# The gate stage dealt out anew and the last stage run tile by tile in a Griffin, sparse-attention and PEER layer

## The chip, the cores and the metric

The kernel runs on one core of a Trainium2 chip. The metric is the time of one execution in device microseconds (us), as the median of several runs. The engines have queues of their own, served in order: TensorE (PE: matrix products into PSUM; PEld is its weight load), VectorE (DVE), ScalarE (ACT: activation functions, copies), GpSimd (POOL) and SyncE (SP, which here only issues transfers). One engine waits for another only through semaphores.

## The reference

One decoder layer over 512 tokens of width 1024, in float32, cut here to the parts around the change:

```
xa  = causal_dwconv(z_rx) + b                      # 4 taps
r   = sigmoid(xa @ w_r + b_r);  ig = sigmoid(xa @ w_i + b_i)     # 8 diagonal blocks of 128
a   = exp(-8 r softplus(-lam))
u   = sqrt(1 - a^2) * (ig * xa)                    # "gate product": ig * xa
h_t = a_t h_(t-1) + u_t                            # scan over the tokens
y_a = (h * gelu(z_rg)) @ w_a
kc, vc = two-layer MLP over blocks of 32 tokens, hidden width 256    # compressed keys, values
...                                                # attention, merge, PEER expert FFN
gate = sigmoid(rmsnorm(h) @ ple_wg)
h    = h + gate * (p @ ple_wp)
out  = rmsnorm(h) * g_final
```

## The kernel before

Every matrix product is made of three (`mm3`): both operands are split into a high part (a copy, rounded) and a low part (the value less its high part), and high x high, high x low and low x high are summed in PSUM. So each weight tile costs a copy and a subtraction before TensorE may use it (`split`, lines 124 to 129: the high part on ScalarE unless an engine is given, the low part on VectorE or GpSimd).

The order of the work is written by hand: the program emits instructions in the order of the Python code, and each engine runs its own in that order. Four stages matter here.

1. **Gate stage, rx chunks (line 398).** Eight chunks of 128 columns of `z_rx`, 24 products each, and then two of `z_kc`. `ev_rx` evacuates a chunk: the convolution on ScalarE (`xa`, line 380) and three VectorE steps (line 382), the splits of the gate weights (`lwhl`) and of `xa` (`xhl`). It hands back `gates`, which `gemm` calls behind the products of the next chunk and ahead of that chunk's evacuation: six products, two sigmoids, and the gate product `gx * xa` (line 395).
2. **Gate stage, rg and vc chunks (lines 547 to 564).** Ten chunks, 24 products each. Between them stand the 32 steps of the compression MLP, 16 for keys and 16 for values (`compress`, lines 480 to 508, products `hid`), at the places that the table `CSTEP` gives: by chunk, the numbers k after which a step comes. Their weights come 256 KB at a time through four buffers (`w1_load`, issued by GpSimd), are cast on ScalarE (`w1_split`, line 455) and get their low half on VectorE (`w1_lo`, line 464), which in turn lets the load four steps on start. `SIDE` gives the places of the work that TensorE does not wait for at once: `lru_b` (tanh and two exponentials), `lru_sqrt`, `lru_c` (product and scan) and the sine and cosine for the rotary embedding.
3. **vs and vw (lines 578 to 605).** The value projections; the last seven steps of the MLP stand in the first of them. `lru_d` follows in the side list.
4. **Last stage (lines 1501 to 1525).** After the expert sums (`va`, in PSUM) the four tiles of 128 tokens are added to the residual (`fin_a`), normalised (`fin_n`), transposed (`fin_t`), multiplied with `ple_wg` in two halves of 512 columns (`fin_mm`, weights `wg0`, `wg1`), gated (`fin_post`), and normalised again for the output (`fin_c`, and by hand for tile 2, which is last). Tile 3 (`GT`) comes first; its part of the FFN was computed by gathers.

Of the kernel before, what the change touches and what calls it, by code (L numbers as in the profile page):

```python
# [94 lines left out]
def tile_hybrid(ctx, tc, a, out, dbg=None):  # L95
# [480 lines left out]
    for br, n in enumerate(("vs", "vw")):  # L576
        hl = hls[br]
        os = [bank("v") for _ in range(NT)]
        for i in range(NT):
            ts = slice(i * 128, (i + 1) * 128)  # L580
            for k in range(KD):
                T.matmul(os[i][:, :256], nhi[:, k, ts], hl[0][:, k], start=k == 0, stop=False)
                T.matmul(os[i][:, :256], nlo[:, k, ts], hl[0][:, k], start=False, stop=False)
# [15 lines left out]
        for i in range(NT):  # L599
# [818 lines left out]
    def fin_post(i, hf, o):
        c = slice(hf * 512, (hf + 1) * 512)
        sgm = wp2.tile([128, 512], F32, name="sgm", tag="sgm", bufs=2)  # L1420
        A.activation(sgm, o, AF.Sigmoid)
# [184 lines left out]
```

## Time and profile before

| | us |
|---|---|
| three runs | 1884.24, 1883.34, 1878.03 |
| their median | 1883.34 |
| the profiled execution | 1883.07 |
| its span, first to last instruction | 1881.3 |
| TensorE busy in the span | 1811.3 (96%) |
| VectorE, ScalarE, GpSimd busy | 1405.0, 840.0, 643.6 |

The span is cut below into stretches by what TensorE does: the rx and kc chunks (24.94 to 90.88 us from its start), rg chunks 0 to 5 with the key MLP (to 137.61), the vc chunks and rg 6 and 7 (to 173.08), vs and vw (to 202.44), everything up to the last expert product (to 1820.69), and the last stage. In rows with brackets the bracket is the idle time of that engine just before the instruction, and what ended it. "x4" is a run of four instructions, and its time is that of all four.

### The profile page before, as it was taken

The page shows a single profiled execution, that of the slowest core. Times are in us where ns is not written, and L with a number is a line of the kernel's source. Part 1 is how long each engine was busy: PE and PEld are TensorE (multiplying, and loading weights), DVE is VectorE, ACT ScalarE, POOL GpSimd, SP SyncE. Part 2 cuts the span into 40 slices and gives each one's busy share as a digit, 9 for nine tenths or more (in the row PEclk, how much of TensorE's full clock was granted, in tenths as well). Part 3 has the DMA queues.
Part 4 walks back from the last instruction along what each step waited for, and adds up shares of the span by engine and source line. Part 5 has one row for each costly group of instructions (what it writes and reads, how often), then busy time and mean ns, then how long its engine had stood idle before and what let it go on. Part 6 is the DMA issues. An engine that isn't in the chain of part 4 may idle for free.

```text
span 1881.3 us, 26477 instructions
## 1 busy us (share of the span) xinstructions
PE 1811.3 (96%) x9817; PEld 1586.6 (84%) x9817; DVE 1405.0 (75%) x2628; ACT 840.0 (45%) x1274; POOL 643.6 (34%) x417
## 2 busy tenths in 40 slices
PE   7998999999999989899999999999999999999997
PEld 6777888778789889899999888888888899999986
DVE  6867616766634388999999957888787788888864
ACT  4464323445522344674765753333333333333443
POOL 3311444322135315435335312222222355555400
PEclk9999999999999999999999999999999999999999
DMA  4353232211015436796897989999999899999941
GB/s 172 102 178 108 79 112 68 68 57 46 23 67 191 181 117 215 260 353 240 293 343 249 355 322 316 356 352 357 344 358 347 306 337 324 354 337 346 358 179 45
DMA packets 179810, 433.29 MB, mean 230 GB/s; under 512 B 14560, under 2 KB 88032, under 8 KB 179680
## 3 DMA queue, kind: packets, MB, share of 16 engines
q1 hardware_dynamic: 119664, 241.96, 37.4%
q0 software_dynamic: 40288, 145.77, 21.8%
q10 hardware_dynamic: 19728, 43.86, 6.1%
q8 instruction: 77, 1.26, 0.3%
q14 instruction: 53, 0.43, 0.1%
HBM read 382.25 MB, written 49.28 MB: 229 GB/s over the span
## 4 chain that ended last, share of the span: by engine, by line
PE 70%; DVE 16%; ACT 4%; issue 4%; DMA 4%; POOL 0%; SPq 0%; DVEq 0%; ACTq 0%; POOLq 0%
PE va L134 9%; PE va L133 9%; PE va L132 9%; PE xu L134 7%; PE xu L132 7%; PE xu L133 7%; DVE ul L1101 2%; DVE oh L1273 2%; DVE gr L1302 2%; PE G L1250 1%; DVE P L769 1%; DMA w1buf<-in_cmp_w 1%; DVE acc L1308 1%; PE z_w_a L134 1%; PE z_w_b L133 1%
## 5 line engine op out<-in xcount | busy, mean ns | idle before, releaser
L132 PE MATMUL xu<-x2hi,uh 128*128 128x384 f32 x1008 | 344.3, 342 | 4.5 <-ACT ac L1111 4.5
L134 PE MATMUL xu<-x2hi,ul 128*128 128x384 f32 x1008 | 339.9, 337 | 6.5 <-DVE ul L1101 6.5
L133 PE MATMUL xu<-x2lo,uh 128*128 128x384 f32 x1008 | 339.2, 337 | 0.0
L132 PE MATMUL va<-v,A 128*128 128x512 f32 x768 | 299.0, 389 | 1.5 <-ACT A L126 1.5
L134 PE MATMUL va<-v,A 128*128 128x512 f32 x768 | 298.9, 389 | 0.0
L133 PE MATMUL va<-v,A 128*128 128x512 f32 x768 | 298.9, 389 | 0.0
L1287 POOL DMA_INDIRECT gr<-in_peer_u,eidx x128 | 170.2, 1329 | 329.5 <-DVE gr L1302 251.7
L1287 POOL DMA_INDIRECT gr<-in_peer_v,eidx x128 | 187.1, 1461 | 268.1 <-DVE acc L1308 210.4
L126 ACT CAST v<-vring 128x1024 fp32r<-128x1024 f32 x128 | 134.7, 1052 | 263.3 <-issue 157.2
L129 DVE TENSOR_TENSOR v<-vring,v 128x1024 fp32r<-128x1024 f32 x128 | 156.4, 1222 | 68.6 <-ACT v L126 68.2
L134 PEld LDWEIGHTS xu<-x2hi,ul 128*128 128x128 f32 x1008 | 190.6, 189 | 7.8 <-DVE ul L1101 7.8
L132 PEld LDWEIGHTS xu<-x2hi,uh 128*128 128x128 f32 x1008 | 190.7, 189 | 6.7 <-ACT ac L1111 5.1
L133 PEld LDWEIGHTS xu<-x2lo,uh 128*128 128x128 f32 x1008 | 190.8, 189 | 1.6
L134 PEld LDWEIGHTS va<-v,A 128*128 128x128 f32 x768 | 144.1, 188 | 30.3 <-DVE A L129 0.6
L132 PEld LDWEIGHTS va<-v,A 128*128 128x128 f32 x768 | 144.1, 188 | 30.2 <-ACT A L126 1.8
L133 PEld LDWEIGHTS va<-v,A 128*128 128x128 f32 x768 | 144.2, 188 | 28.5 <-DVE v L129 0.3
L1308 DVE SCALAR_TENSOR_TENSOR acc<-gr,dots,acc 128x1024 f32<-128x1024 f32 x128 | 163.8, 1280 | 1.6
L1302 DVE SCALAR_TENSOR_TENSOR gr<-gr,x2g 128x1024 f32<-128x1024 f32 x128 | 158.0, 1254 | 8.2 <-DMA gr<-in_peer_u,eidx 8.2
L1096 ACT CAST uh<-ur 128x1024 fp32r<-128x1024 f32 x126 | 132.6, 1053 | 57.3 <-ACT ac L1111 29.7
L1111 ACT ACTIVATE ac<-xu 128x384 f32<-128x384 f32 x128 | 63.7, 498 | 191.7 <-PE xu L134 181.8
L1101 DVE TENSOR_TENSOR ul<-ur,uh 128x1024 fp32r<-128x1024 f32 x100 | 121.4, 1220 | 17.6 <-PE xu L134 8.3
L1253 ACT ACTIVATE gst<-G 128x512 f32<-128x512 f32 x96 | 100.3, 1158 | 13.5 <-PE G L1250 13.2
(449 smaller groups left out, 3599.5 us busy)
## 6 DMA issues: line engine op xcount, KB each, us to landing
vring<-in_peer_v SPq DMA_DIRECT2D x128, 512.0 KB
ur<-in_peer_uT SPq DMA_DIRECT2D x126, 512.0 KB
gdram<-gst ACTq DMA_DIRECT2D x12, 2048.0 KB
gt<-gdram SPq DMA_DIRECT2D x32, 768.0 KB
xdram<-ac ACTq DMA_DIRECT2D x88, 192.0 KB
vring<-xdram SPq DMA_DIRECT2D x88, 192.0 KB
raw_m<-in_w_in SPq DMA_DIRECT2D x16, 512.0 KB
raw_rx<-in_w_in SPq DMA_DIRECT2D x8, 512.0 KB
```

The costliest lines, as they stand in the source:

```text
L126: A.copy(hi, src)
L129: (eng or V).tensor_tensor(lo, src, f(hi), op=OP.subtract)
L132: T.matmul(o, sh, mh, start=start, stop=False)
L133: T.matmul(o, sh, ml, start=False, stop=False)
L134: T.matmul(o, sl, mh, start=False, stop=stop)
L1096: A.copy(us[e][0], urs[e])
L1101: (G if search[0] else V).tensor_tensor(us[e][1], urs.pop(e), f(us[e][0]), op=OP.subtract)
L1111: A.activation(ac, o[:, :ND], AF.Gelu_apprx_tanh)
L1253: A.activation(gst[:, :, c:c + 4].rearrange("p a t -> p t a"), o.rearrange("p (t a) -> p t a", t=4), AF.Copy, scale=1.0 / GSC)
L1287: G.indirect_dma_start(out=r, out_offset=None, in_=tab, in_offset=bass.IndirectOffsetOnAxis(ap=eidx[:, j:j + 1], axis=0))
L1302: V.scalar_tensor_tensor(r, r, 1.0, x2g, op0=OP.mult, op1=OP.mult, accum_out=dots[:, j:j + 1])
L1308: V.scalar_tensor_tensor(acc, r, dots[:, j:j + 1], acc, op0=OP.mult, op1=OP.add)
```

## The change

The gate product is no longer part of `gates`: it is put in a list `late`, which the next chunk's `ev_rx` empties behind its own convolution and splits (the last one goes into the side list). `CSTEP` and `SIDE` are new tables. At the end of a chunk that is followed by one with MLP steps, the low halves of all weights cast so far are made. In the last stage the four steps add, statistic, normalise and transpose go tile by tile, with the last quarter of `wg1`'s second half split between the tiles; the square root's table is loaded ahead; tile 0 is transposed after the fourth of eight steps of the product before it and not after the seventh; and tile 2's last product is made in two of 256 columns, with the multiplication by `g_final` ahead of the last statistic.

```diff
+    late = []
...
-        split(wh[:, 0], wh[:, 1], w, G, V)
-        split(xh[:, 0], xh[:, 1], xa)
+        A.copy(xh[:, 0], xa)
+        V.tensor_copy(wh[:, 0], w)
+        V.tensor_tensor(xh[:, 1], xa, f(xh[:, 0]), op=OP.subtract)
+        G.tensor_tensor(wh[:, 1], w, f(wh[:, 0]), op=OP.subtract)
+        while late:
+            late.pop(0)()
 
         def gates():
...
-            V.tensor_tensor(gx[:, c], gx[:, c], xa, op=OP.mult)
+            late.append(lambda: V.tensor_tensor(gx[:, c], gx[:, c], xa, op=OP.mult))
         return gates
...
+    side.insert(0, lambda: late.pop(0)())
...
-    gemm([("kc", i, nhi, nlo, ev_kv(0)) for i in range(2)], nside=(2, 1), nxt=[("rg", 0), ("rg", 1)])
+    gemm([("kc", i, nhi, nlo, ev_kv(0)) for i in range(2)], nside=(3, 1), nxt=[("rg", 0), ("rg", 1)])
...
-    CSTEP = [(), (), (1, 3, 5, 7), (1, 3, 5, 7), (1, 3, 5, 7), (0, 2, 3, 5, 7), (), (), (4, 5, 6, 7), (0, 1, 3, 4, 6, 7)]
-    SIDE = [(5,), (), (), (0, 0), (0, 0), (1,), (0, 0, 4), (0, 3, 6), (1, 2, 5), (1, 4, 6)]
+    CSTEP = [(), (), (1, 3, 5, 7), (1, 3, 5, 7), (1, 3, 5, 7), (0, 2, 3, 5, 7), (), (), (1, 6, 7), (0, 1, 2, 4, 5, 6, 7)]
+    SIDE = [(5,), (), (), (2, 4), (2, 4), (2,), (0, 0, 3, 6), (3, 6), (7, 7), (5,)]
...
             run_side(SIDE[n].count(k))
+            if k == 7 and CSTEP[n + 1:n + 2] != [()]:
+                w1_lo(w1n[1])
...
                 if br == 0 and k % 4 == 3:
                     next(comp, None)
+                if br == 0 and i < 3 and k == 5:
+                    run_side(1)
...
-            run_side(1)
+            run_side(1 + br)
...
-            if mid is not None and k == 6:
+            if mid is not None and k == midk:
                 mid()
...
-            w_half(wg1, 1, raw_p7)
+            for k in range(0, KD - 2, 2):
+                w_part(wg1, 1, k, raw_p7)()
+            wcut = w_part(wg1, 1, KD - 2, raw_p7)
+            A.activation(rms[:, 3, 1:2], rms[:, 2, 1:2], AF.Sqrt)
...
-    for i in range(GT):
-        fin_a(i)
-    fin_n(range(GT))
-    og = [fin_mm(GT, 0, "o"), fin_mm(GT, 1, "f", lambda: fin_t(0, ("ax", "ax")))]
+    fin_a(0)
+    fin_a(1)
+    rms_fin(0, 1)
+    fin_a(2)
+    apply3(0)
+    rms_fin(1, 2)
+    wcut()
+    apply3(1)
+    rms_fin(2, 3)
+    apply3(2)
+    og = [fin_mm(GT, 0, "o"), fin_mm(GT, 1, "f", lambda: fin_t(0, ("ax", "ax")), 3)]
...
+    ends = [(0, 512), (512, 768), (768, 1024)]
+    for n, (c0, c1) in enumerate(ends):
+        fin_post(2, c0 // 512, fin_mm(2, c0 // 512, cols=(c0 % 512, (c1 - 1) % 512 + 1)), (c0, c1))
+        if n == 2:
+            A.activation(rms[:, 3, 1:2], rms[:, 2, 1:2], AF.Sqrt)
+        A.activation(last[:, c0:c1], h2[:, c0:c1], AF.Square, accum_out=sq[:, n:n + 1])
+        if n == 1:
+            V.tensor_tensor(sq[:, 0:1], sq[:, 0:1], sq[:, 1:2], op=OP.add)
+        V.tensor_tensor(h2[:, c0:c1], h2[:, c0:c1], gF[:, c0:c1], op=OP.mult)
+    V.tensor_tensor(sq[:, 2:3], sq[:, 2:3], sq[:, 0:1], op=OP.add)
     rms_fin(2, 3)
+    A.activation(last[:, :512], h2[:, :512], AF.Copy, scale=rms[:, 3, 2:3])
+    V.tensor_scalar(last[:, 512:], h2[:, 512:], rms[:, 3, 2:3], None, op0=OP.mult)
```

First place: VectorE in the rx chunks, from one weight cast (`w`, for a chunk two ahead) to the split of `xa`. Before:

```order
L128 CAST w_555<-raw_kc 128x1024
L395 TENSOR_TENSOR gx<-gx,xa 128x512
L382 SCALAR_TENSOR_TENSOR xa<-z_rx,par,xa 128x511
L382 SCALAR_TENSOR_TENSOR xa<-z_rx,par,xa 128x510
L382 SCALAR_TENSOR_TENSOR xa<-z_rx,par,xa 128x509
L128 CAST lwhl<-lruw 128x256
L129 TENSOR_TENSOR xhl<-xa,xhl 128x512
```

Now:

```order
L128 CAST w_555<-raw_kc 128x1024
L384 SCALAR_TENSOR_TENSOR xa<-z_rx,par,xa 128x511
L384 SCALAR_TENSOR_TENSOR xa<-z_rx,par,xa 128x510
L384 SCALAR_TENSOR_TENSOR xa<-z_rx,par,xa 128x509
L390 CAST lwhl<-lruw 128x256
L391 TENSOR_TENSOR xhl<-xa,xhl 128x512
L401 TENSOR_TENSOR gx<-gx,xa 128x512
```

The gate product of the chunk before has moved from ahead of the convolution to behind the split.

Second place: VectorE where the MLP steps begin (rg chunk 2) and go on (chunk 3); `w` are the weights of a chunk two ahead, `w1hl` the MLP's low halves, `tt` the vector part of `lru_b`. Before:

```order
L129 TENSOR_TENSOR w_819<-raw_rg,w_819 128x1024
L128 CAST w_850<-raw_rg 128x1024
L129 TENSOR_TENSOR w_850<-raw_rg,w_850 128x1024
L464 TENSOR_TENSOR w1hl<-w1buf,w1hl 128x512 x2
L464 TENSOR_TENSOR w1hl<-w1half,w1hl 128x512 x2
L464 TENSOR_TENSOR w1hl<-w1buf,w1hl 128x512
L128 CAST w_915<-raw_rg 128x1024
L129 TENSOR_TENSOR w_915<-raw_rg,w_915 128x1024
L410 SCALAR_TENSOR_TENSOR tt<-a_805,tt 128x512
L410 SCALAR_TENSOR_TENSOR tt<-a_922,tt 128x512
L464 TENSOR_TENSOR w1hl<-w1buf,w1hl 128x512
```

Now:

```order
L129 TENSOR_TENSOR w_819<-raw_rg,w_819 128x1024
L471 TENSOR_TENSOR w1hl<-w1buf,w1hl 128x512
L128 CAST w_852<-raw_rg 128x1024
L129 TENSOR_TENSOR w_852<-raw_rg,w_852 128x1024
L471 TENSOR_TENSOR w1hl<-w1buf,w1hl 128x512
L471 TENSOR_TENSOR w1hl<-w1half,w1hl 128x512 x2
L471 TENSOR_TENSOR w1hl<-w1buf,w1hl 128x512 x2
L128 CAST w_917<-raw_rg 128x1024
L129 TENSOR_TENSOR w_917<-raw_rg,w_917 128x1024
L417 SCALAR_TENSOR_TENSOR tt<-a_805,tt 128x512
L471 TENSOR_TENSOR w1hl<-w1half,w1hl 128x512
L417 SCALAR_TENSOR_TENSOR tt<-a_935,tt 128x512
```

One low half now stands ahead of each chunk's weight cast and subtraction, and the `tt` steps stand between low halves and not ahead of them.

Third place: VectorE at the program's end, tile 2's last 512 columns and the output. Before:

```order
L1422 TENSOR_TENSOR sgm<-sgm,ppb 128x512
L1423 TENSOR_TENSOR h<-h,sgm 128x512
L1520 TENSOR_TENSOR rms<-rms 128x1
L286 TENSOR_SCALAR rms<-rms 128x1
L287 RECIPROCAL rms<-rms 128x1
L1524 SCALAR_TENSOR_TENSOR x3s<-h,rms,gfinB 128x512 x2
```

Now (from the product with `g_final` of the first 512 columns on):

```order
L1549 TENSOR_TENSOR h<-h,gfinB 128x512
L1434 TENSOR_TENSOR sgm<-sgm,ppb 128x256
L1435 TENSOR_TENSOR h<-h,sgm 128x256
L1548 TENSOR_TENSOR rms<-rms 128x1
L1549 TENSOR_TENSOR h<-h,gfinB 128x256
L1434 TENSOR_TENSOR sgm<-sgm,ppb 128x256
L1435 TENSOR_TENSOR h<-h,sgm 128x256
L1549 TENSOR_TENSOR h<-h,gfinB 128x256
L1550 TENSOR_TENSOR rms<-rms 128x1
L286 TENSOR_SCALAR rms<-rms 128x1
L287 RECIPROCAL rms<-rms 128x1
L1553 TENSOR_SCALAR x3s<-h,rms 128x512
```

Six instructions have become twelve; the two fused output steps have become products ahead of the statistic and one scaling behind it, with the other half of the scaling on ScalarE.

## Rows read from the trace of the kernel before

**Rows 1.** The busy time by stretch: bounds in us, length, busy time of PE, PEld, DVE, ACT and POOL (instructions), granted TensorE clock, share of the DMA engines, GB/s.

```profile
24.94:90.88 65.94, 62.48 (x265) 49.08 (x264) 54.28 (x104) 28.62 (x41) 27.38 (x20) 1.00 0.35 111
90.88:137.61 46.73, 42.27 (x210) 34.44 (x209) 31.65 (x45) 31.95 (x49) 9.12 (x17) 1.00 0.57 177
137.61:173.08 35.47, 30.02 (x137) 24.23 (x136) 31.37 (x42) 19.07 (x26) 3.97 (x8) 0.90 0.35 109
...
202.44:1820.69 1618.25, 1586.40 (x8704) 1400.89 (x8702) 1228.81 (x2342) 712.96 (x1074) 585.05 (x359) 1.00 0.70 248
1820.69:1836.66 15.97, 12.68 (x59) 9.96 (x58) 10.71 (x16) 8.27 (x12) 0.00 (x0) 1.00 0.37 145
1871.06:1881.30 10.24, 0.16 (x1) 0.00 (x0) 4.66 (x9) 3.62 (x9) 0.00 (x0) 0.64 0.26 102
```

**Rows 2.** The timeline of TensorE in the rx and kc chunks: start, duration, engine, line, operation, shapes, count.

```profile
24.94 0.39 PE L132 MATMUL z_rx<-nhi,w 128*128 128x512 f32 x1
...
30.38 0.39 PE L132 MATMUL lru<-xhl,lwhl 128*128 128x512 f32 x1
...
60.77 0.49 PE L132 MATMUL lru<-xhl,lwhl 128*128 128x512 f32 x1 [1.21 <-ACT xhl L126]
61.62 0.50 PE L133 MATMUL lru<-xhl,lwhl 128*128 128x512 f32 x1 [0.36 <-DVE xhl L129]
```

**Rows 3.** The timeline of GpSimd (one row, a low half of `w`) and VectorE in the same chunks.

```profile
54.84 2.40 POOL L129 TENSOR_TENSOR w<-raw_rx,w 128x1024 fp32r<-128x1024 f32 x1 [2.76 <-DVE w L128]
...
54.88 2.91 DVE L395 TENSOR_TENSOR gx<-gx,xa 128x512 f32<-128x512 f32 x1
57.71 2.30 DVE L382 SCALAR_TENSOR_TENSOR xa<-z_rx,par,xa 128x511 f32<-128x511 f32 x3
...
76.52 2.13 DVE L270 SCALAR_TENSOR_TENSOR ang<-kt,ang 128x512 f32<-128x512 f32 x3
...
79.63 0.68 DVE L395 TENSOR_TENSOR gx<-gx,xa 128x512 f32<-128x512 f32 x1
```

**Rows 4.** The timeline of TensorE and VectorE in rg chunk 2.

```profile
104.57 0.62 PE L491 MATMUL hid<-w1hl,blk 128*124 128x256 f32 x3 [1.16 <-DVE w1hl L464]
108.26 0.64 PE L491 MATMUL hid<-w1hl,blk 128*124 128x256 f32 x4
110.11 0.64 PE L491 MATMUL hid<-w1hl,blk 128*124 128x256 f32 x4
...
103.83 1.28 DVE L464 TENSOR_TENSOR w1hl<-w1buf,w1hl 128x512 fp32r<-128x512 f32 x2
```

**Rows 5.** The busy time of rg chunks 3 and 4, from one gelu on ScalarE to the next (columns as in Rows 1; ScalarE's is the fourth busy time).

```profile
110.50:121.10 10.60, 9.28 (x48) 7.31 (x47) 7.04 (x11) 9.83 (x16) 2.68 (x5) 1.00 0.51 149
121.10:131.66 10.56, 8.59 (x46) 6.80 (x45) 6.17 (x9) 9.33 (x15) 2.15 (x4) 1.00 0.53 161
```

**Rows 6.** The timeline around the MLP's weight loads: the issue on GpSimd, the casts and the gelu on ScalarE.

```profile
104.81 1.14 POOL L449 DMA_DIRECT2D w1buf<-in_cmp_w  x2 [18.79 <-DVE w1hl L464]
...
109.31 1.29 ACT L455 CAST w1hl<-w1buf 128x512 fp32r<-128x512 f32 x2 [5.21 <-DMA w1buf<-in_cmp_w]
...
120.60 0.60 ACT L527 ACTIVATE gr<-z_rg 128x512 f32<-128x512 f32 x1
```

**Rows 7.** The timeline of TensorE and VectorE around rg chunk 6, where the MLP for the values begins.

```profile
154.47 0.74 PE L491 MATMUL hid<-w1hl,blk 128*124 128x256 f32 x4 [1.27 <-DVE blk L129]
...
159.06 1.00 PE L491 MATMUL hid<-w1hl,blk 128*124 128x256 f32 x3 [3.04 <-DVE w1hl L464]
...
141.71 0.69 DVE L420 TENSOR_TENSOR gx<-gx,tt 128x512 f32<-128x512 f32 x1 [1.94 <-ACT tt L415]
142.43 1.23 DVE L421 TENSOR_TENSOR_SCAN rr<-rr,gx 128x512 f32<-128x512 f32 x1
...
158.34 0.67 DVE L464 TENSOR_TENSOR w1hl<-w1buf,w1hl 128x512 fp32r<-128x512 f32 x1
```

**Rows 8.** The timeline of the last stage up to the first product of tile 0: VectorE, ScalarE, TensorE.

```profile
1824.73 1.22 DVE L129 TENSOR_TENSOR wg<-wgr,wg 128x1024 fp32r<-128x1024 f32 x1 [2.82 <-ACT wg L126]
1825.87 3.67 DVE L1395 TENSOR_TENSOR h<-va,h 128x512 f32<-128x512 f32 x6
1832.33 3.68 DVE L291 SCALAR_TENSOR_TENSOR x3s<-h,rms,gpleB 128x1024 f32<-128x1024 f32 x3 [1.14 <-ACT rms L288]
...
1830.79 1.28 ACT L288 ACT_TABLE_LOAD   x1
...
1833.67 1.09 PE L297 MATMUL xT<-cst,x3s 128*128 128x128 f32 x8 [2.55 <-DVE x3s L291]
...
1836.66 0.50 PE L134 MATMUL pg<-wg,x3lo 128*128 128x512 f32 x1 [0.74 <-DVE x3lo L129]
```

**Rows 9.** The timeline of the end: tile 2's two sigmoids and the last transfer's issue on ScalarE, and on VectorE a product of 512 columns and, from further up, a subtraction of 256.

```profile
1870.49 0.60 ACT L1421 ACTIVATE sgm<-pg 128x512 f32<-128x512 f32 x1
...
1873.26 0.58 ACT L1421 ACTIVATE sgm<-pg 128x512 f32<-128x512 f32 x1
...
1878.34 0.34 ACTq L1525 DMA_DIRECT2D out<-x3s  x1
...
1871.12 0.69 DVE L1422 TENSOR_TENSOR sgm<-sgm,ppb 128x512 f32<-128x512 f32 x1 [0.62 <-ACT sgm L1421]
...
206.53 0.42 DVE L129 TENSOR_TENSOR vv<-v,vv 128x256 fp32r<-128x256 f32 x1
```

More of the change, by code (lines that the diff above doesn't have):

```diff
@@ L1374, in v_mm @@
                 mm3(va[i][hf], A2[:, 0, ts], A2[:, 1, ts], v[:, 0, c], v[:, 1, c], e == 0, e == NE - 1)
-    def w_half(dst, hf, raw):
-        for k in range(0, KD, 2):
-            w_part(dst, hf, k, raw)
     def w_part(dst, hf, k, raw):
@@ L1382, in w_part, with cut @@
         SP.dma_start(r, a["ple_wg"][k * 128:(k + 2) * 128, hf * 512:(hf + 1) * 512].rearrange("(k p) c -> p k c", p=128))
-        split(dst[:, 0, k:k + 2], dst[:, 1, k:k + 2], r)
+        def cut():
+            split(dst[:, 0, k:k + 2], dst[:, 1, k:k + 2], r)
+        return cut
     def wgr(n):
@@ L1406, in fin_t, with fin_mm @@
         dump("h2_%d" % i, hs[i])
-    def fin_mm(i, hf, tag="ax", mid=None):
+    def fin_mm(i, hf, tag="ax", mid=None, midk=6, cols=(0, 512)):
         w = (wg0, wg1)[hf]
@@ L1412, in fin_mm, with fin_post @@
         for k in range(KD):
-            mm3(o, x3hi[:, k, ts], x3lo[:, k, ts], w[:, 0, k], w[:, 1, k], k == 0, k == KD - 1)
-            if mid is not None and k == 6:
+            mm3(o[:, :cols[1] - cols[0]], x3hi[:, k, ts], x3lo[:, k, ts], w[:, 0, k, cols[0]:cols[1]],
+                w[:, 1, k, cols[0]:cols[1]], k == 0, k == KD - 1)
+            if mid is not None and k == midk:
                 mid()
         return o
[L1418 to L1421, printed above, removed]
+    def fin_post(i, hf, o, cols=None):
+        c0, c1 = cols or (hf * 512, (hf + 1) * 512)
+        c = slice(c0, c1)
+        sgm = wp2.tile([128, 512], F32, name="sgm", tag="sgm", bufs=2)[:, :c1 - c0]
+        A.activation(sgm, o[:, :c1 - c0], AF.Sigmoid)
         V.tensor_tensor(sgm, sgm, ppb[:, i, c], op=OP.mult)
@@ L1489, in tile_hybrid @@
         if e >= NE - 12 and e % 2 == 0 and e < NE - 4:
-            w_part(wg0, 0, e - NE + 12, wgr)
+            w_part(wg0, 0, e - NE + 12, wgr)()
         if e == NE - 2:
@@ L1514, in tile_hybrid @@
     fin_c([GT, 0, 1])
-    fin_b(2, 0)
-    A.activation(last[:, :512], hs[2][:, :512], AF.Square, accum_out=rms[:, 0, 0:1])
-    fin_b(2, 1)
-    A.activation(rms[:, 3, 1:2], rms[:, 2, 1:2], AF.Sqrt)
-    A.activation(last[:, 512:], hs[2][:, 512:], AF.Square, accum_out=rms[:, 0, 2:3])
-    V.tensor_tensor(rms[:, 0, 2:3], rms[:, 0, 2:3], rms[:, 0, 0:1], op=OP.add)
+    h2, sq = hs[2], rms[:, 0]
+    ends = [(0, 512), (512, 768), (768, 1024)]
[8 more added lines that the diff above has]
+    V.tensor_tensor(sq[:, 2:3], sq[:, 2:3], sq[:, 0:1], op=OP.add)
     rms_fin(2, 3)
+    A.activation(last[:, :512], h2[:, :512], AF.Copy, scale=rms[:, 3, 2:3])
+    V.tensor_scalar(last[:, 512:], h2[:, 512:], rms[:, 3, 2:3], None, op0=OP.mult)
     for hf in range(2):
         c = slice(hf * 512, (hf + 1) * 512)
-        V.scalar_tensor_tensor(last[:, c], hs[2][:, c], rms[:, 3, 2:3], gF[:, c], op0=OP.mult, op1=OP.mult)
-        (SP, A)[hf].dma_start(out[GT * 128 - 128:GT * 128, c], last[:, c])
+        (A, SP)[hf].dma_start(out[GT * 128 - 128:GT * 128, c], last[:, c])
     leave(p7cm)
```

2 lines of the change are left out of this document (added).

## The prediction

> **What bounds the kernel now.** The busy time by stretch comes first [rows 1]: from 202.44 to 1820.69 us TensorE is busy 1586.40 of 1618.25, and no other engine comes near. The change touches nothing there, so a microsecond won ahead of it moves everything behind it forward. TensorE waits in the stage ahead, and at the end.
>
> Busy time hides part of a wait, so I count products. 24 products lie between 24.94 and 30.38 [rows 2]: 0.227 each. A step of the MLP with six products takes 110.11 - 108.26 = 1.85 undisturbed [rows 4], so the step itself is 1.85 - 1.36 = 0.49.
> - rx and kc: 264 products are 59.9; the stretch took 65.9. Lost: 6.0.
> - rg 0 to 5: 144 products and 16 steps are 32.7 + 7.8 = 40.5; it took 46.7. Lost: 6.2.
> - vc, rg 6 and 7: 96 products, nine steps and some 0.3 for a small product are 26.5; it took 35.5. Lost: 9.0. Of these three only here is the granted clock under 1.00: 0.90, part of the stretch at the lower of its two levels, after waits of 1.27 and 3.04 [rows 1, 7].
> - In the last stage TensorE waits 2.55 for tile 0's normalised values and 0.74 for their low half [rows 8], and from 1871.06 it has nothing to do for 10.24 [rows 1].
>
> **rx chunks.** What TensorE waits for is a chain: two sigmoids and the convolution's first part on ScalarE, 2.30 of convolution on VectorE, the split of xa. The gate product stands ahead of the convolution. It takes 0.68 alone, and 2.91 when GpSimd is subtracting: GpSimd's 2.40 begins at 54.84, the product at 54.88, and the product ends 0.55 behind GpSimd [rows 3]. The convolution that follows is 2.2 late; TensorE then waits 1.21 and 0.36 [rows 2]. The product moved behind the split leaves the convolution free to start with ScalarE's part. A chunk has 30 products, 6.8; the chain without the late start just fits. What stays: the sine's argument (2.13, [rows 3]) and a weight cast stand ahead of the eighth convolution as before; the product only changed sides there. With the start-up and smaller scalar steps I leave 1.7 of the 6.0. Gain 4.3, bounds 3 (half as much again left) and 6.0 (all).
>
> On that lock: in the Trainium skill, "SBUF — State Buffer", section "Who interferes with whom", a VectorE instruction with two SBUF inputs and a GpSimd instruction that reads SBUF exclude each other for a whole instruction. The 2.91 agrees. By this rule the product could pay it again at its new place only if GpSimd were subtracting there; its next subtraction follows a cast that now comes after the product, so the sum is the same by rule and by row.
>
> **rg 0 to 5.** Before, each chunk's low halves stand behind a weight cast and subtraction that wait for TensorE to free a buffer; the second product of a step then waits, 1.16 at 104.57 for the low half begun at 103.83 [rows 4]. Now one is ready when the chunk begins, and loads are issued earlier too. That removes the waits at the first steps. But ScalarE is the second bound: in chunks 3 and 4 it is busy 9.83 + 9.33 = 19.2 [rows 5], while TensorE needs 4 x 1.85 = 7.4 each, 14.8. Of these 19.2, a table load (1.28, as in [rows 8]) and a gelu (0.60, [rows 6]) at the end hold up no weight: 17.3. So 2.5 stays lost however the pieces are dealt out: lru_b's parts now stand between the casts and not in front of them, but none is dropped. Gain 6.2 - 2.5 = 3.7. Bounds: 0, if a load that takes 4.5 from issue to cast (104.81 to 109.31, [rows 6]) starts ScalarE's row of work later by as much, and 6.2, if its queue runs far enough ahead of TensorE.
>
> **vc, rg 6 and 7.** VectorE is the bound: it waits for the square root until 141.71 [rows 7] and then works on to the low half at 158.34, which TensorE awaited for 3.04. That low half now stands ahead of the second vc chunk's split, and the step itself comes a product group later. Following VectorE's new order with product and scan at 0.69 + 1.23 = 1.9, and the rest at their old durations, I find four waits left: 1.4 at the first value step (its input is 0.6 later behind that low half, less what the table change gives), 1.7 where a low half stands behind sine, product and scan, 1.2 behind the split of the vs weights, 0.7 behind another product and scan. Together 5.0, none as long as 3.04, so I count the clock as staying at its upper level. Gain 4.0; bounds 0 (the lows only change places in a full queue) and 9.0. Three scans move into vs, beside products whose stretch I did not find waiting on VectorE for long: I take 0, bounds -1 and +1.
>
> **Last stage, to tile 0's first product.** Before, VectorE waits 2.82 for the last weights until 1824.73, and only then adds six times (3.67) [rows 8]. Now the additions start where that wait began, 1821.9, and are done at 1825.6; with a statistic in between tile 0 is normalised from 1826.1 to 1827.4 and not behind three tiles' statistics from 1832.33. Its transposes come after 12 products of the current 24 and not 21, at 1828.9: no wait. The weights' cast and low half come between tiles 0 and 1, until 1830.3, before TensorE needs them at 1831.1. The split of tile 0 is late instead: on ScalarE it stands behind tile 2's square root, on VectorE behind tile 2's normalisation; I get 1834.0 for the low half against 1836.66. Gain 2.6, bounds 0 (ScalarE's two queues of small steps run 2.6 later than worked out) and 3.3 (both waits gone).
>
> The table load at 1830.79 [rows 8] leaves the path: VectorE went on at 1832.33, so load and square root cost 1.54. "ScalarE: Activation LUTs" in the Trainium skill, "What ACT_TABLE_LOAD costs", adds a drain, about 2.7 a switch. No drain shows here; by the page this part would gain 1.4 more as an estimate, were the load alone on the path.
>
> **The end.** What bounds it is not TensorE but the alternation of ScalarE and VectorE: sigmoid, two products or sums, square, and only then the next sigmoid. From 1870.49 to the last transfer's issue at 1878.34 it is 7.85, with 2.77 from sigmoid to sigmoid for 512 columns [rows 9]. Now there are three pieces. A VectorE step of 256 columns is 0.42 against 0.69 [rows 9], not half. First piece 2.8 as before; second 2.2 (0.4 + 0.45 + 0.45 + 0.55, and 0.35 because the product with g_final, which must wait for the square, stands ahead); third 2.4 to its square's sum (the table load of 1.28 ends 0.3 behind the sum it waits for); statistic and square root 1.2; scaling on ScalarE 0.6. That is 9.2: 1.35 longer. Halving TensorE's last product gains nothing: before, its products end at 1871.06 [rows 1] and the second sigmoid starts at 1873.26 [rows 9], so the chain is late against TensorE already. Bounds: -0.3 (the wait behind the square and the table load cost nothing) and 2.2.
>
> **Sum.** 4.3 + 3.7 + 4.0 + 0 + 2.6 - 1.35 = 13.2, against the profiled execution's 1883.07 (span 1881.3 and 1.77 around it), which lies 0.27 under the median shown. Forecast 1870. Its own range, with the terms' bounds taken as unlikely to fall together: 1865 to 1876.
>
> **Rivals.**
> - *The second bound holds everywhere.* ScalarE in rg 3 and 4 and VectorE in rg 6 and 7 have no less work than before (31.95 and 31.37 busy, [rows 1]); dealt out anew, the waits only move. Then the two rg terms give about 1 together: 1883.07 - 4.3 - 1 - 1.25 = 1876.5. For it: those sums. Against it: the longest wait, 3.04, and the lower clock come from one order that is gone.
> - *All waits go.* No engine's work reaches a stretch's length [rows 1], so a good order could hide it all: 6.0 + 6.2 + 9.0 + 1.25 = 22.5, 1860.5. Against it: 2.5 on ScalarE and the fixed places of the scans.
> - *Slower: the loads become the pace.* Every load waits for a low half four steps back. A loop of four steps is load, cast (0.65), low half (0.64) and three handovers, 1.6 and the load: with 4.5, 1.5 a step, under TensorE's 1.85. VectorE now stands at a chunk's end until the newest cast is done, and all weight splits queue behind it. Lost against 1.85 on 16 steps and 1.7 on nine, it eats up the 15.2 lost before and the other gains of 5.6 from 2.6 a step on, a load of 9. At 10 the time would be 1890. Against it: the 4.5, and transfer engines busy only 0.57 and 0.35 of these stretches [rows 1].
>
> **How the numbers follow.** Forecast 0.62; second bound 0.17; all waits go 0.17; slower 0.04. Three runs of before spread over 6 us, and 0.3% (5.65, to 1877.7) is about what a measurement of this kernel tells from no change. Faster than that: 0.62 less 0.02, 0.17, and 0.09 of the second bound's 0.17, 0.86; within it 0.11; slower 0.03. The range holding 8 in 10 reaches into the two neighbours: 1863 to 1878.
>
> **What would show it.** In the profile after: no wait over 0.4 at the gates' products but one near the eighth chunk, and no gate product over 1 us; first MLP step without a wait, waits of 1 to 2 near the ends of rg 4; granted clock 1.0 up to vs; ks beginning near 190.5; tile 0's first low product 2.6 earlier against the last expert product; and over 9 us from tile 2's first sigmoid to the last issue. It is wrong if the MLP waits move to the loads, if the clock falls again, or if the middle stretch does not keep its 1618.

## The result, and the profile after

The changed kernel takes 1871.4 us (median of six runs, 1868.15 to 1873.14) against 1882.13 for the kernel before beside it (1878.03 to 1884.24): ratio 0.9939, 95% interval 0.9927 to 0.9951. The forecast was 1870.0 with a range of 1863 to 1878. The profiled execution took 1873.14, of which 1871.4 is its span, 9.9 shorter than the span before.

The busy time by stretch of the changed kernel, cut at the same first products as [rows 1]: rx chunk 1 to rg, rg 0 to 5, vc with rg 6 and 7, vs and vw (in [rows 1] not shown: 29.36 before), the long stretch, the last stage up to tile 0's first low product, and from the end of the last product to the end of the span (10.08 before, by the same cut).

```profile
25.59:87.38 61.79, 61.13 (x266) 49.14 (x264) 50.12 (x104) 28.64 (x41) 25.85 (x20) 1.00 0.36 116
87.38:132.89 45.51, 43.59 (x210) 35.64 (x209) 31.95 (x46) 32.26 (x49) 10.12 (x17) 0.96 0.59 186
132.89:163.98 31.09, 27.64 (x137) 22.56 (x136) 27.68 (x38) 17.62 (x22) 4.04 (x8) 1.00 0.38 116
163.98:194.80 30.82, 29.32 (x238) 28.25 (x237) 18.55 (x27) 12.21 (x24) 11.48 (x8) 1.00 0.30 100
194.80:1812.31 1617.51, 1585.87 (x8704) 1400.68 (x8702) 1226.29 (x2342) 714.37 (x1075) 586.44 (x359) 1.00 0.70 248
...
1859.95:1871.40 11.45, 0.00 (x1) 0.00 (x0) 4.98 (x14) 4.59 (x12) 0.00 (x0) 0.58 0.21 84
```

The columns are read against [rows 1]: the third stretch went from 35.47 to 31.09 and its granted clock from 0.90 to 1.00; the second only from 46.73 to 45.51, with its clock down to 0.96; vs and vw grew by 1.46. By stretch the gains are 4.15, 1.22, 4.38, -1.46 and 0.74, then 2.89 up to the end of the last product (50.53 to 47.64) and -1.37 behind it. They add up to 10.55; 0.65 was lost ahead of all that (rx chunk 1 begins at 25.59, not 24.94).

In the rx chunks, VectorE's gate product and convolution and GpSimd's subtraction in the changed kernel, at the place of [rows 3]:

```profile
54.93 2.40 POOL L129 TENSOR_TENSOR w<-raw_rx,w 128x1024 fp32r<-128x1024 f32 x1 [3.37 <-DVE w L128]
...
55.07 2.32 DVE L384 SCALAR_TENSOR_TENSOR xa<-z_rx,par,xa 128x511 f32<-128x511 f32 x3 [0.22 <-ACT xa L382]
58.88 0.68 DVE L401 TENSOR_TENSOR gx<-gx,xa 128x512 f32<-128x512 f32 x1
```

The convolution now runs beside the subtraction, each at its own length, and the product comes behind both. All eight products take 0.68 or 0.69. The waits of [rows 2] are gone; one of 0.56 is left at the eighth chunk's gates.

TensorE at the last MLP step of rg 4, the first of rg 5 and the steps around rg 6 and 7, to be read beside [rows 4, 7]:

```profile
121.45 0.38 PE L498 MATMUL hid<-w1hl,blk 128*124 128x256 f32 x1 [0.42 <-ACT w1hl L462]
122.18 0.62 PE L498 MATMUL hid<-w1hl,blk 128*124 128x256 f32 x3 [0.34 <-DVE w1hl L471]
123.96 0.38 PE L498 MATMUL hid<-w1hl,blk 128*124 128x256 f32 x1 [0.46 <-ACT w1hl L462]
124.69 1.00 PE L498 MATMUL hid<-w1hl,blk 128*124 128x256 f32 x3 [0.35 <-DVE w1hl L471]
...
150.33 0.73 PE L498 MATMUL hid<-w1hl,blk 128*124 128x256 f32 x4 [1.17 <-DVE blk L129]
...
155.52 0.62 PE L498 MATMUL hid<-w1hl,blk 128*124 128x256 f32 x3 [1.33 <-DVE w1hl L471]
...
160.48 0.62 PE L498 MATMUL hid<-w1hl,blk 128*124 128x256 f32 x3 [0.51 <-DVE w1hl L471]
...
163.53 0.61 PE L498 MATMUL hid<-w1hl,blk 128*124 128x256 f32 x3 [0.45 <-DVE w1hl L471]
```

At the end of rg 4 and the start of rg 5 four small waits follow each other, at each step first for ScalarE's cast and then for VectorE's low half. Behind them the three products at 124.69 last 1.00 in place of 0.62: the granted clock was at its lower level (0.50) for about 3 us. From gelu to gelu ScalarE is now busy 9.24 of 9.35 and 9.25 of 9.37 in chunks 3 and 4 ([rows 5]: 9.83 of 10.60, 9.33 of 10.56):

```profile
107.02:116.37 9.35, 9.01 (x48) 7.32 (x47) 6.82 (x10) 9.24 (x14) 2.42 (x4) 1.00 0.59 170
116.37:125.74 9.37, 7.80 (x37) 5.87 (x36) 5.72 (x9) 9.25 (x14) 2.65 (x5) 0.93 0.54 171
```

TensorE in the last stage up to tile 0's first low product ([rows 8]), and ScalarE at the end ([rows 9]):

```profile
1820.54 1.03 PE L297 MATMUL xT<-cst,x3s 128*128 128x128 f32 x8
1825.17 0.50 PE L134 MATMUL pg<-wg,x3lo 128*128 128x512 f32 x1 [0.39 <-DVE x3lo L129]
...
1858.90 0.60 ACT L1433 ACTIVATE sgm<-pg 128x512 f32<-128x512 f32 x1
...
1868.01 0.34 ACTq L1556 DMA_DIRECT2D out<-x3s  x1
```

Tile 0's transposes have no wait, and 0.39 is left at its low product. From tile 2's first sigmoid to the last issue it is 9.11, 1.26 more than in [rows 9].

### The profile page after: what moved, and what is told of

Same layout as the page of the kernel before. It is cut to its first block, busy times and chain, and to the rows that moved or that the text cites. A ratio compares the mean times of both kernels' runs of the same rounds, so it can differ in the third digit from the quotient of the medians.

```text
span 1871.4 us, 26544 instructions
## 1 busy us (share of the span) xinstructions
PE 1808.8 (97%) x9841; PEld 1587.3 (85%) x9841; DVE 1399.5 (75%) x2637; ACT 842.0 (45%) x1281; POOL 645.1 (34%) x417
## 3 DMA queue, kind: packets, MB, share of 16 engines
q8 instruction: 77, 1.26, 0.3%
## 5 line engine op out<-in xcount | busy, mean ns | idle before, releaser
L1264 ACT ACTIVATE gst<-G 128x512 f32<-128x512 f32 x96 | 100.4, 1162 | 13.2 <-PE G L1261 12.9
```

Source lines behind the costliest of these rows:

```text
L1264: A.activation(gst[:, :, c:c + 4].rearrange("p a t -> p t a"), o.rearrange("p (t a) -> p t a", t=4), AF.Copy, scale=1.0 / GSC)
```

## The experiments

All were run beside the kernel before. Ratios are against it in the same session.

| run | time, median (runs) | ratio, 95% interval |
|---|---|---|
| e1_gate | 1878.12 (10) | 0.9966, 0.9957 to 0.9976 |
| e2_mlp | 1873.93 (4) | 0.9947, 0.9930 to 0.9963 |
| e3_last | 1883.66 (10) | 1.0000, 0.9990 to 1.0010 |
| e4_oldtail | 1871.15 (4) | 0.9932, 0.9914 to 0.9950 |
| e5_lrub | 1869.45 (4) | 0.9935, 0.9917 to 0.9953 |
| e6_nolead | 1873.42 (4) | 0.9952, 0.9933 to 0.9971 |
| e7_oldtab | 1878.39 (10) | 0.9975, 0.9962 to 0.9988 |
| e8_early | 1870.89 (4) | 0.9940, 0.9921 to 0.9959 |
| e9_lowv | 1882.72 (8) | 1.0001, 0.9991 to 1.0012 |
| e10_latescan | 1869.46 (4) | 0.9917, 0.9901 to 0.9934 |
| e11_both | 1866.42 (4) | 0.9902, 0.9885 to 0.9918 |
| e12_all | 1863.63 (5) | 0.9897, 0.9877 to 0.9917 |

One execution of a kernel differs from the next by up to 5 us and more, so the whole time seldom decides a question of 1 us here. The lengths of the stretches do. Where an edit does not touch them and the clock does not fall, rx repeats within 0.1, vc with rg 6 and 7 within 0.25, and rg 0 to 5 within 0.55. One stretch falls out of this, the rx chunks of e2_mlp; it is taken up with e9_lowv.

**The three parts alone.** e1_gate is the kernel before with the gate product behind the split (the hunks on `late`), e2_mlp with the two tables, the lows ahead and the scans in vs, e3_last with the last stage.

> The kernel before with the first part of the change alone: the gate product behind the next chunk's split, nothing else. Theory (the product beside GpSimd's subtraction made the convolution late, and TensorE waited for it): from rx chunk 1's first product to rg's first product 65.94 before, 61.8 now as in the changed kernel; all later stretches keep their lengths of before (rg and vc 82.2, vs and vw 29.4, end 10.1); time 4.2 under before, 1878. Rival (the MLP's loads and VectorE's queue set when vs begins, whatever the rx chunks take): rg and vc get longer by what rx won, and the time stays within 1 of before.

> The kernel before with the second part alone: the new tables of MLP steps and side work, the low halves a chunk ahead, three scans in vs. Theory (the two parts are independent): rg and vc 82.2 before, 76.6 as in the changed kernel, of which chunks rg 0 to 5 45.5; vs and vw 30.8 against 29.4 before; rx stays 65.9; net 4.1 under before, 1878. Rival (a part of the gain of rg comes only because VectorE enters the stage earlier with the gate products moved): rg and vc 78 or more, time within 2.5 of before.

> The kernel before with the last stage alone: tile by tile, halved last product, new end. Theory: first product of the last stage to the end of its last 50.53 before, 47.6 now; from there to the end of the span 10.1 before, 11.45 now; net 1.5 under before, 1880.6. Rival (the halved product is what shortens the products' stretch, and the tile order does nothing): the stretch to tile 0's first low product is unchanged at 16.

The busy time by stretch: of e1_gate, rx and kc; of e2_mlp, rg 0 to 5 and vs with vw.

```profile
24.86:86.65 61.79, 61.12 (x265) 49.17 (x264) 50.15 (x104) 28.63 (x41) 26.50 (x20) 1.00 0.37 116
```

```profile
93.93:137.43 43.50, 41.94 (x210) 34.45 (x208) 31.64 (x45) 32.20 (x49) 10.12 (x17) 1.00 0.59 186
168.50:198.57 30.07, 29.05 (x239) 28.16 (x238) 18.55 (x27) 12.24 (x24) 11.49 (x8) 1.00 0.30 92
```

e1_gate has the 61.79 of the changed kernel to the hundredth, and behind it the lengths of before (82.31, 29.37): the first part stands by itself. e2_mlp has rg 0 to 5 at 43.50 with the clock at 1.00, so the 45.51 of the changed kernel's profile holds some 1.9 that belong to that execution, its clock above all, and not to the change. vs and vw are 0.7 longer than before, not 1.46. One expected number failed: e2_mlp's rx chunks took 68.38 and not 65.9, though nothing was edited there. Both times lie further under before than expected (5.7 and 9.9, against 4.2 and 4.1); the edited stretches give 4.2 and 7.6 - 0.7. By the medians the three parts add up to 15.8, while the whole change gained 10.7 in its own session; the stretches do not show that difference, and its cause is open.

e3_last shows no difference in time, though its last stage takes 47.70 + 11.41 = 59.11 against 60.61 in the profile before. The reason lies in before: its last stage is not always 60.61. e1_gate and e2_mlp have the old one, and there it took 49.31 and 49.29, with 10.08 behind the last product in both. TensorE and VectorE in that stage of e1_gate, with the rows of before in [rows 8]:

```profile
1830.20 1.09 PE L297 MATMUL xT<-cst,x3s 128*128 128x128 f32 x8 [1.33 <-DVE x3s L291]
1833.19 0.50 PE L134 MATMUL pg<-wg,x3lo 128*128 128x512 f32 x1 [0.74 <-DVE x3lo L129]
...
1821.27 1.22 DVE L129 TENSOR_TENSOR wg<-wgr,wg 128x1024 fp32r<-128x1024 f32 x1 [1.60 <-ACT wg L126]
```

VectorE waited 1.60 for the last weights, not 2.82, and TensorE 1.33 for tile 0, not 2.55. So the part's own worth, halved product included, was 1.5 against one execution and 0.2 to 0.3 against two others. With the old order tile 0's low product came 15.97, 14.74, 14.72 and (e9_lowv) 14.30 behind the stage's first product, as the load of the last weights took 6.9 to 5.2 from its issue to the cast; in all ten profiles with the new order it came after 12.85 to 12.87. The new order no longer waits for that load.

**The end.** e4_oldtail is the changed kernel with the old end:

```diff
-    ends = [(0, 512), (512, 768), (768, 1024)]
...
+    fin_b(2, 0)
+    A.activation(last[:, :512], hs[2][:, :512], AF.Square, accum_out=rms[:, 0, 0:1])
+    fin_b(2, 1)
```

> The changed kernel with the end of before: tile 2's second half as one product of 512 columns, the product with g_final last. Theory (the third piece makes the alternation of ScalarE and VectorE longer, and TensorE is not what bounds there): from tile 2's first sigmoid to the last issue 7.85 as before, not 9.11; end of the last product to the end of the span 10.1 and not 11.45; all else as in the changed kernel; 1.3 under it, 1870. Rival (the halving lets the last chain start earlier and the longer end only repays that): the end comes within 0.3 of the changed kernel's.

ScalarE in the end of e4_oldtail:

```profile
1859.65 0.60 ACT L1433 ACTIVATE sgm<-pg 128x512 f32<-128x512 f32 x1
...
1867.49 0.34 ACTq L1550 DMA_DIRECT2D out<-x3s  x1
```

7.84 from the first sigmoid to the last issue, and 10.07 behind the last product against 11.45: the theory's numbers. The time cannot tell 1.3 (0.9932 beside 0.9939). Here rg 0 to 5 took 43.67 at clock 1.00, as in e2_mlp.

**What binds in rg 3 and 4.** e5_lrub issues the activations of three channels in chunk 0, VectorE's share staying where it was:

```diff
-            if c < 8:
-                a2s[c] = t2("a2")
+            for d in {3: (3, 4, 5), 4: (), 5: (), 8: ()}.get(c, (c,)):
+                a2s[d] = t2("a2")
```

> The changed kernel with the two exponentials and the tanh of channels 4 and 5 issued beside channel 3's in rg chunk 0, where ScalarE already has that table, and not in chunk 3. Theory (ScalarE is the second bound in chunks 3 and 4): its busy time there falls by two table loads of 1.28 and six activations of 0.72, chunk 3 has no wait and chunk 4 half of its own or less; rg 0 to 5 take 41.5 to 42.5 against 43.67 (45.51 in the profile in which the clock fell), and the granted clock stays at 1.00 in the stretch; later stretches as before. Time about 1.5 under the changed kernel, 1870. Rival (the weight loads set the pace of those steps): ScalarE waits for the loads instead, rg 0 to 5 stay above 43.

```profile
87.12:129.28 42.16, 41.43 (x209) 34.47 (x208) 31.77 (x46) 29.67 (x47) 10.10 (x17) 1.00 0.59 189
```

42.16: ScalarE's busy time fell by two table loads (32.26 to 29.67), TensorE's two waits that are left of the four, at the first step of chunk 5, are 0.39 and 0.34, and the clock stayed. The four profiles with this edit lie between 42.11 and 42.65, under the 43.50 and 43.67 without it. ScalarE was the bound. (ScalarE itself now waits for loads, up to 3.00 at the start of chunk 3, and TensorE waits for none of them there.)

**Low halves ahead, or the tables?** Each is taken out of the changed kernel by itself: e6_nolead drops the two lines

```diff
-            if k == 7 and CSTEP[n + 1:n + 2] != [()]:
-                w1_lo(w1n[1])
```

and e7_oldtab keeps them and has the two tables of before, without scans in vs.

> The changed kernel without the low halves made ahead at a chunk's end. Theory (the waits at the first MLP steps came from the low half behind a weight split, and making it ahead removed them): those waits come back, about 1.3 each, at chunks 2, 3 and 4, and rg 0 to 5 take 46 to 47 against 43.67; in chunk rg 6, where the step's low half again stands behind the vc split, a wait of about 3. Rival (the new tables removed them, by putting the side work elsewhere): rg 0 to 5 within 0.7 of 43.67.

> The changed kernel with the tables of before for MLP steps and side work (and no scans in vs), and the low halves made ahead as now. Theory: rg 0 to 5 gain most of what they gain in all, 44 to 44.7 against 43.67 with the new tables and 46.7 before; vc, rg 6 and 7 take 33 to 34, between 31.1 and 35.4, since the step that waited 3.2 for its low half no longer does, but the other waits of the order stay; vs and vw 29.4 as before, since no scan stands there. Rival (tables do it all): 46.7 and 35.4.

e6_nolead took 44.98 in rg 0 to 5 and 31.47 in vc, rg 6 and 7, with the clock at 1.00. One wait came back (1.16, at the second product of chunk 2's first step, as in [rows 4]), not three, and not the long one. e7_oldtab, by stretch as above, and TensorE and ScalarE at its third step of chunk 3:

```profile
86.36:132.99 46.63, 43.03 (x210) 35.56 (x209) 31.99 (x45) 32.43 (x49) 9.39 (x17) 0.96 0.55 179
132.99:168.26 35.27, 28.72 (x137) 23.73 (x136) 31.40 (x42) 18.71 (x24) 4.05 (x8) 0.95 0.33 110
```

```profile
112.02 0.57 PE L498 MATMUL hid<-w1hl,blk 128*124 128x256 f32 x1 [2.10 <-ACT w1hl L462]
...
106.71 1.28 ACT L414 ACT_TABLE_LOAD   x1
...
111.37 1.12 ACT L462 CAST w1hl<-w1half 128x512 fp32r<-128x512 f32 x2
```

The 46.63 and 35.27 are the numbers of e7_oldtab's rival (tables do it all). But the clock fell behind that wait, and by the spacing of the products that ran at the lower level it took 1.3; without it the first stretch would be 45.3, an estimate. So both runs agree: the lows ahead are worth 1.3 in rg 0 to 5 (44.98 - 43.67, and 46.7 - 45.3) and the tables the other 1.7; in vc, rg 6 and 7 the tables give 3.8 to 4.2 and the lows 0.4 at most (35.27, 31.47, 31.08). Both theories missed: the lows did less than half in rg 0 to 5 and next to nothing behind it. The rows show why the lows alone do little. With the old table two channels' activations and a table load stand ahead of the cast on ScalarE, and where TensorE no longer waits for a low half it waits 2.10 for the cast; around rg 6 the long wait even became 3.72.

**The lock and the place.** e9_lowv is the kernel before with `lo_eng[0] = V` ahead of the rx chunks.

> The kernel before with the low half of each rx weight made on VectorE and not on GpSimd; the gate product stays ahead of the convolution. Theory (the product is long because GpSimd's subtraction of the same moment holds it up, and only that makes the convolution late): every gate product takes 0.68 to 0.72, the waits at the gates' products in chunks 4 and 5 fall from 1.2 and 1.4 to under 0.5, and from rx chunk 1's first product to rg's first product it is 62.5 to 64 against 65.94, though VectorE has 1.23 more a chunk. Rival (the place ahead of the convolution is what costs, whatever the product's length): the waits stay, and the extra 1.23 makes it 66 or more.

```profile
25.47:91.62 66.15, 62.87 (x265) 49.01 (x264) 57.52 (x111) 28.62 (x41) 8.34 (x12) 1.00 0.31 101
```

Of before's eight products three were long: 2.08, 2.91 and 2.09. Here all eight took 0.68 or 0.69 at the same place, so the length came from GpSimd. But the stretch stayed at 66.15, which is the rival's number: with 1.23 more a chunk on VectorE the convolution is as late as before (TensorE's waits for the gates' products come to 3.3 in sum, against 3.5, with 1.03 as the longest, in the eighth chunk). Since it lengthens the same queue, this run cannot split the 4.15 between the lock and the place ahead of the convolution.

The chunks of before and of the changed kernel can. These stretches hold the chunks of the products of 2.08 and 2.91, before and after:

```profile
45.84:62.88 17.04, 14.75 (x61) 11.11 (x60) 14.31 (x28) 5.33 (x9) 6.25 (x4) 1.00 0.28 86
...
46.63:60.32 13.69, 13.69 (x62) 11.19 (x60) 10.91 (x29) 5.34 (x9) 6.30 (x4) 1.00 0.31 100
```

Together with the chunk of the 2.09 (8.11 to 6.83) the three became 4.6 shorter. The rest, where the product was short at its old place, is 0.5 longer now (the chunk from 62.88 took 6.93 and takes 7.10). So the 4.15 come from the products that GpSimd held up; ahead of the convolution a short product cost nothing.

Which product is long was decided by a few tenths of a microsecond. The rows are GpSimd's subtraction and VectorE's fifth product, first in before and then in e2_mlp, whose rx chunks have the same instructions:

```profile
64.18 2.78 POOL L129 TENSOR_TENSOR w<-raw_rx,w 128x1024 fp32r<-128x1024 f32 x1 [3.17 <-DVE w L128]
64.02 0.68 DVE L395 TENSOR_TENSOR gx<-gx,xa 128x512 f32<-128x512 f32 x1
...
64.80 2.38 POOL L129 TENSOR_TENSOR w<-raw_rx,w 128x1024 fp32r<-128x1024 f32 x1 [3.16 <-DVE w L128]
64.89 2.84 DVE L395 TENSOR_TENSOR gx<-gx,xa 128x512 f32<-128x512 f32 x1 [0.17 <-ACT gx L394]
```

In before the product began 0.16 ahead of the subtraction, and the subtraction took 2.78 in place of 2.40; in e2_mlp it began 0.09 behind, and took 2.84 itself. What made it late there was TensorE's clock: behind waits of 1.20 and 0.35, which before has as well, it was granted 0.50 from 63 to 66 us, the gates' products came late, and with them the second sigmoid. The fall and the fourth long product together made the 68.38.

**The end again.** In e8_early the statistics of tiles 3, 0 and 1 are taken as each tile is done, their roots stand together ahead of tile 2's first sigmoid, and tile 1's scaling behind it:

```diff
-    fin_c([GT, 0, 1])
+    fin_s(1)
+    for i in (GT, 0, 1):
+        rms_fin(i, i + 1)
+    fin_o(GT)
+    fin_o(0)
...
+        if n == 0:
+            fin_o(1)
```

> The changed kernel with the statistics of tiles 3, 0 and 1 at the end taken as soon as each tile is done and their square roots together ahead of tile 2's first sigmoid, and the last of their scalings behind it; the three pieces of tile 2 stay. Theory (the end is the alternation of ScalarE and VectorE, and it starts late because tile 2's first sigmoid stands behind those statistics: TensorE has its product done 4.6 earlier): the first sigmoid starts within 1.5 of its last product, the last sigmoid within 0.7 of TensorE's last product and not 3.9 after it; end of the last product to the end of the span 8.2 to 8.8 against 11.45; time 3 under the changed kernel, 1868.5. Rival (the alternation itself is as long as TensorE's three products): less than 1 won.

```profile
1867.74 0.36 ACT L1433 ACTIVATE sgm<-pg 128x256 f32<-128x256 f32 x1
```

The last product ends at 1867.27: the last sigmoid follows it by 0.47, and 8.03 remain behind it, 3.4 less than in the changed kernel. The median of the time (1870.89) does not show it; the profiled execution had the longest long stretch of all, 1625.78, and a fall of the clock in rg 0 to 5 (45.08 at 0.96). Where the edit was joined to e5_lrub, below, the ratio is 0.9902 against 0.9935.

**The scans in vs, and all together.** e10_latescan is e5_lrub with

```diff
-                if br == 0 and i < 3 and k == 5:
-                    run_side(1)
+                if br == 0 and i == 3 and k == 5:
+                    run_side(3)
```

> The kernel of e5_lrub with the three scans of the vs stretch together behind the last MLP steps instead of between them. Theory (a product and scan ahead of a low half makes TensorE wait 0.93 there): that wait goes, and vs and vw take 29.3 to 29.6 against 30.1; all else as e5_lrub, 0.6 under it. Rival (the loads pace the steps there): the waits move to the next casts, and vs and vw stay at 30 or more.

```profile
161.03:190.20 29.17, 28.82 (x239) 28.19 (x237) 19.45 (x27) 12.24 (x24) 11.77 (x8) 1.00 0.28 91
```

29.17, 0.9 to 1.1 under e4_oldtail (30.10) and e5_lrub (30.23), and no longer than before: the wait of 0.76 behind the scans is gone, so the scans between the steps were that cost.

e11_both joins e5_lrub and e8_early, puts tile 2's second sigmoid ahead of its first square and drops the in-place product with g_final for the second half; e12_all adds the late scans.

> The changed kernel with the exponentials of e5_lrub and the early statistics of e8_early, and in the end the second piece's sigmoid ahead of the first piece's square, no in-place product with g_final for the second half (its scaling takes it along). Theory (both gains add, since one is ahead of the long stretch and one behind it): rg 0 to 5 42.2; end of the last product to the end of the span 7.2 to 7.7, against 11.45 in the changed kernel and 8.03 in e8_early; time 3.3 + 3.8 = 7 under the changed kernel's profile of 1873.1, by the median 1865. Rival (the long stretch takes back what starts earlier): 1869 or more.

> The kernel of e11_both with the late scans of e10_latescan. Theory (independent stretches, so their gains add): rg 0 to 5 42.2 to 42.7, vs and vw 29.2, end of the last product to the end of the span 7.7; 0.9 under e11_both, 1865.5 by the median, if the long stretch takes its 1617.5 to 1622. Rival (the long stretch grows when it starts earlier): its length above 1622 and the time at 1867 or more.

e12_all by stretch, cut as above, from vs on (rg 0 to 5 took 42.11):

```profile
159.89:188.36 28.47, 28.47 (x238) 28.04 (x237) 19.52 (x27) 12.29 (x24) 11.64 (x8) 1.00 0.28 91
188.36:1804.70 1616.34, 1584.49 (x8704) 1399.28 (x8703) 1227.12 (x2343) 712.83 (x1075) 584.64 (x360) 1.00 0.70 248
1852.38:1860.10 7.72, 0.00 (x0) 0.00 (x0) 2.40 (x8) 3.19 (x7) 0.00 (x0) 0.78 0.35 136
```

e11_both had 42.36 and 7.70 where it was expected, and 1866.42, between the theory's 1865 and the rival's 1869. e12_all takes 1863.63, ratio 0.9897 (0.9877 to 0.9917): by the ratios it beats both kernels. vs and vw took 28.47, where 29.2 was expected: one load there reached its cast 4.14 behind its issue, in e10_latescan 4.72, and TensorE waited for nothing. The long stretch was 1616.34 here, where it starts earliest, so it does not take back what the front wins.

## Why the prediction was right, and where it was not

The time lay within the range and 1.4 above the forecast. The terms, in the order of its sum:

- **rx, 4.3: right.** 4.15 in the changed kernel and in e1_gate; 1.9 stays lost where 1.7 was left. The signs held: eight products under 1, one wait near the eighth chunk. On the lock: the product slowed only beside GpSimd (before and e9_lowv), and the chunks in which it did so gave the whole gain. The Trainium skill, "SBUF — State Buffer", section "Who interferes with whom", holds two SBUF inputs to be its condition; the convolution, whose z_rx lies in PSUM, agrees with it at 2.32 beside GpSimd's 2.40.
- **rg 0 to 5, 3.7: the bound right, one reason wrong.** With the clock undisturbed it is 3.1 to 3.2 (43.67 and 43.50), so 3.0 to 3.2 stay lost where 2.5 was left; e5_lrub shows that ScalarE was that bound. In the profiled execution only 1.22 came, because the clock fell near 125 behind the four waits at the end of chunk 4: the sign "granted clock 1.0 up to vs" failed there. The step that failed is "That removes the waits at the first steps", said of the low halves. Before, only chunk 2's wait stood at a first step (1.16); it depends on them (e6_nolead) and is worth 1.3. In chunks 3 and 4 the second step waited, as the rows below show for before, and with the old tables and the lows ahead chunk 3's third step waits 2.10 for the cast instead (e7_oldtab). The tables gave the rest; by the rows, because the activations on ScalarE and `tt` on VectorE no longer stand in a block ahead of the casts and low halves.

```profile
115.11 0.62 PE L491 MATMUL hid<-w1hl,blk 128*124 128x256 f32 x3 [0.98 <-DVE w1hl L464]
...
125.21 0.62 PE L491 MATMUL hid<-w1hl,blk 128*124 128x256 f32 x3 [1.63 <-DVE w1hl L464]
```

- **vc, rg 6 and 7, 4.0: right.** 4.38. Of the four waits counted as 1.4, 1.7, 1.2 and 0.7 TensorE shows, from start to start less the products, 1.32, 1.49, 0.66 and 0.61; the third, "1.2 behind the split of the vs weights", was sized too high. The clock stayed at 1.00, as counted, but not for the reason given (no wait as long as 3.04): in rg 4 and 5 it fell behind waits of which the longest was 0.46.
- **vs, 0 with bounds of 1: wrong.** -0.7 where nothing else disturbed it, -1.46 in the profile. The failing step is "beside products whose stretch I did not find waiting on VectorE for long": the MLP's steps run in that stretch too (before, one waits 0.76 for a low half there), and in the changed kernel VectorE has a product and a scan ahead of the low half that the step at 170.08 waits for. e10_latescan settles it. The other 0.7 goes with a weight load: issued at 160.97, cast at 166.24 when its data came, 5.27 and not the 4.5 of [rows 6]. That is the rival of the loads in small, in one stretch.

```profile
160.97 1.07 POOL L456 DMA_DIRECT2D w1half<-in_cmp_w  x2 [3.47 <-ACT w1hl L462]
...
166.24 0.62 ACT L462 CAST w1hl<-w1half 128x512 fp32r<-128x512 f32 x1 [4.70 <-DMA w1half<-in_cmp_w]
...
168.22 1.23 DVE L428 TENSOR_TENSOR_SCAN rr<-rr,gx 128x512 f32<-128x512 f32 x1
...
170.08 0.62 PE L498 MATMUL hid<-w1hl,blk 128*124 128x256 f32 x3 [0.76 <-DVE w1hl L471]
```

- **Last stage, 2.6: its mechanism right, its base was one execution.** From the first product to tile 0's low product it went from 15.97 to 12.86, 3.1 earlier; against e1_gate and e2_mlp (14.74 and 14.72) it is 1.9, against e9_lowv 1.4. VectorE's 2.82 for the last weights was taken for a property of the kernel; it is 1.60 in e1_gate and 1.15 in e9_lowv.
- **The end, -1.35: right.** -1.26 by the sigmoids, and e4_oldtail gives it back. (The products of before end at 1871.22, 0.16 behind the 1871.06 of the working; nothing hangs on it.) What the working passed over is that the chain starts late: not TensorE's last product but the statistics of three other tiles held tile 2's first sigmoid, and e8_early takes 3.4 out there.
- **The long stretch** was to keep its 1618: 1617.51. That was partly luck: over the thirteen other profiles of this study it took 1616.34 to 1625.78, with no relation to when it began.

Of the sum of 13.2, the profiled execution gave 9.9; the 3.3 are 2.5 in rg 0 to 5, 1.5 in vs, 0.15 in rx and 0.65 of the start, less 0.4 in vc and 0.74 of the long stretch and 0.3 in the last stage (rounded). So the sign "ks beginning near 190.5" failed too: it began at 194.80. The rivals "second bound" and "all waits go" both failed: rg and vc gave 5.6 together where the one allowed 1 and the other 15.2.

## What to carry to other kernels

A wait names the instruction that came last, not the one to move: with the low halves made a chunk earlier one wait went and another went over to the cast ahead of it, until ScalarE's queue was dealt anew. Work moved out of a crowded stretch is not free where it lands, if the stretch that receives it still holds the tail of the same chain: look for steps of that chain there before writing zero. And a wait for a transfer in one profile is one draw; before a term rests on it, compare it over several executions, and judge edits of 1 us by the length of their stretch, not by the whole time.

## What the runs showed that was not expected

The lower clock level comes and goes between executions of the same code. rg 0 to 5 with the new tables took 45.51 (the changed kernel) and 45.08 (e8_early) with the clock falling behind the waits at chunk 4's end, and 43.67 (e4_oldtail) and 43.50 (e2_mlp) with the same four waits and no fall. The products with w_out (the projection behind the attention) scatter most in the long stretch, from 44.0 to 48.9: in e4_oldtail TensorE waited 3.29 there for a cast of their weights and then ran for some microseconds at the lower level, in before it waited 1.42 without a fall. From the first product with w_out to the next stage's first it was 48.95 against 44.69. The rows are those of TensorE at that wait in e4_oldtail, with the window around it, and in before.

```profile
577.09 0.58 PE L933 MATMUL wo<-w8woh,mhi 128*128 128x256 f32 x1 [3.29 <-ACT w8woh L946]
```

```profile
576.00:584.00 8.00, 6.91 (x37) 6.91 (x37) 0.00 (x0) 3.13 (x3) 7.01 (x3) 0.57 0.45 134
```

```profile
586.20 0.38 PE L922 MATMUL wo<-w8woh,mhi 128*128 128x256 f32 x1 [1.42 <-ACT w8woh L935]
```
